# A two-block transformer forward pass: the second block's modulation vectors as multiply-and-sum instructions on VectorE in the feed-forward parts, in place of matmuls on TensorE in the mixing stages

## The chip, the core and the metric

The kernel runs on one core of a Trainium2 chip. Its engines are named as the profile names them: PE is TensorE (PEld its weight loads), DVE is VectorE, ACT is ScalarE, POOL is GpSimd, SP is SyncE, which here only issues DMAs. Each engine works through one queue of instructions in order; engines wait for one another by semaphores. The metric is the device time of one execution in microseconds (us).

## What is computed

Two transformer blocks on 512 tokens of width 1024, in fp32. The first block has two layers, each a feed-forward, a mixing stage (attention over selected keys, RWKV-7 and a gated delta net side by side) and a second feed-forward. The second block has two layers with adaptive layer norms: latent attention and a feed-forward, then Fourier mixing and a feed-forward. The change concerns the modulation vectors of these norms, which depend on `c` and `c_ctx` (one vector of 1024 each) and on weights alone, not on the tokens:

```python
def ada(cvec, w, b):                       # cvec [1, 1024], w [1024, 6144]
    return jnp.split(jax.nn.silu(cvec) @ w + b, 6, axis=-1)
...
for i in range(DEPTH):                     # DEPTH = 2
    sh1, sc1, g1, sh2, sc2, g2 = [m[:, None, :] for m in ada(c, ada_w[i], ada_b[i])]
    csh1, csc1, cg1, csh2, csc2, cg2 = ada(c_ctx, ada_w[i], ada_b[i])
```

The feed-forward that occurs four times in the first block, and the mixing stage between two of them:

```python
def swiglu(h, w_gate, w_up, w_down):       # 1024 -> 2816 -> 1024
    return (jax.nn.silu(h @ w_gate) * (h @ w_up)) @ w_down
...
x = x + 0.5 * swiglu(rms_norm(x, ffn_norm[l, 0]), ffn_w_gate[l, 0], ffn_w_up[l, 0], ffn_w_down[l, 0])
... # mixing: x = x + concat(ya, yb, yc) @ w_out[l]
x = x + 0.5 * swiglu(rms_norm(x, ffn_norm[l, 1]), ffn_w_gate[l, 1], ffn_w_up[l, 1], ffn_w_down[l, 1])
```

## The kernel before, in words

Activations are kept by feature: a tile has 128 features on the partitions and 512 tokens in a row. Matmuls in fp32 are made of three fp32r matmuls, with each operand split into a high and a low part. `slab` fetches a weight block of 128x1024 (512 KB) into `wraw`, a ring of **three** buffers, by a DMA on SP's queue (L159); ACT casts it to the high part `whi` (L160), DVE subtracts for the low part `wlo` (L161), each in a ring of two; `mm3` issues the three matmuls (L167 to L169). A `wraw` buffer is free when both parts are made, a `whi` or `wlo` buffer when PE has used it.

A feed-forward (`ffn`) first walks over 11 pairs of hidden tiles `f0`, with four slabs for each (the up part, matmuls `pg`); its results are evacuated by DVE and ACT (L292 to L295, split at L172 and L173). Then `down` multiplies back to the width of 1024: two halves of the output, 11 slabs each (the down part, matmuls `pd`, 24 for a slab), and DVE adds each half to `x` (L321 before, L323 after). The first instructions of the following norm (`xh`, `xl` L215, `sq` L253) run as soon as x is ready.

The mixing stage (`Mix`) interleaves generators: `r0`, `r1` (RWKV heads), `g0`, `g1` (delta net), attention tiles and projections. The recurrences end in a chain of state steps: PE multiplies the state by two matrices (`bY` L758, `bS` L761), DVE adds the input of the chunk (`S`, L762), and the next step needs that. `stream(tag, level)` sets the priority with which a scheduler merges the pieces into each engine's queue when the kernel is built; a lower level goes earlier.

`Block2.ada` makes the modulations of one layer, as such a generator (`fill`), called four times late in `Mix`. Each of its first three pieces takes 2048 output features: for each of 8 tiles of input features two DMAs of 512 KB into the `wraw` ring (L1105), straight from the weights and not split, and four fp32 matmuls with the activations as the stationary operand, 128x32 of which two columns count (L1107); then ACT copies the bank (`adt`, L1110). The last piece transposes (`adT`, L1083) and adds the bias.

Of the kernel before, what the change touches and what calls it, by code (L numbers as in the profile page):

```python
# [9 lines left out]
F32 = mybir.dt.float32  # L10
# [71 lines left out]
_QF = [("norm1_g0", 8), ("norm1_g1", 8), ("norm2_g0", 8), ("norm2_g1", 8), ("ada_b0", 48), ("ada_b1", 48), ("cc", 16),  # L82
# [13 lines left out]
class Net:  # L96
    """Buffers and the parts that all layers share. A stream is a run of dependent work with its own buffers: tiles of one tag
    get their buffers in program order, so only work with other tags can go ahead of work that waits."""
# [22 lines left out]
    def phase(self):  # L121
        """what follows comes after all before it in priority."""
        self.base += 400000
        self.next = {}
        self.tc.cur_priority = self.base

    @contextmanager
    def stream(self, tag, level):
        """work with the buffers of tag; the lower its level the sooner an engine takes it."""
        old, pri = self.tag, self.tc.cur_priority  # L130
        key = (tag, level)
        self.tag, self.tc.cur_priority = tag, self.next.get(key, self.base + int(level * 40000))
        yield
        self.next[key] = self.tc.cur_priority
        self.tag, self.tc.cur_priority = old, pri
# [39 lines left out]
    def rsqrt(self, src, n, eps):  # L175
        """(src + eps) ** -0.5 of a [128, n] block: a guess from the bits, a step of third order and one of Newton's."""
# [5 lines left out]
        # t = v y^2, y <- y (t^2 - 10/3 t + 5): 8/3 of the root  # L182
# [4 lines left out]
        # of z = 3/8 y: z (1.5 - 0.5 v z^2)  # L187
# [6 lines left out]
    def rsqrt3(self, src, n, eps):  # L194
        """(src + eps) ** -0.5 of a [128, n] block, by Newton's iteration."""
# [11 lines left out]
    def split_x(self, x, g, level=0.002):  # L207
        """(x * g) in two fp32r parts; the rms factor of x over the features, on all partitions and by token."""
# [14 lines left out]
    def rms(self, acc, ones, nt, eps, tag=None, copy=True):  # L223
        """rsqrt of the mean over the partitions of the sum of acc, [128, nt*128] each: by token, and on all partitions."""
# [31 lines left out]
    def split_mod(self, x, G, sh, w=T, r=None):  # L256
        """rms_norm(x) * G + sh in two fp32r parts."""
# [17 lines left out]
    def ffn(self, x, xs, wg, wu, wd, scale, pre=iter(())):  # L275
# [3 lines left out]
        for f0 in range(0, NF, 2):  # L279
# [9 lines left out]
            for i in range(2):  # L289
# [15 lines left out]
    def down(self, x, hh, hl, w, order, scale, banks=(("a", "a", "x", "x"), ("pj", "pj", "c", "c"))):  # L305
# [19 lines left out]
class Mix:  # L325
    """Sequence mixing of one layer of the first block. Streams: "w" projections, "c" the recurrences one after the other,
    "a" index scores and attention."""

    def __init__(self, net, l, x, par, w_in, lup, v_down, v_up, w_out, vfirst, fill):
# [16 lines left out]
        def go(part, tag="c", level=0):  # L346
            """the next piece of a part."""
# [27 lines left out]
        go(fill, "w", 1.25)  # L375
        go(fill, "w", 4)
# [28 lines left out]
    def proj_fm(self, c0, n=128):  # L405
        """[n, T] of rms_norm(x) @ w_in[:, c0:c0+n]."""
# [9 lines left out]
    def proj_tm(self, c0, evac, tiles=range(4)):  # L416
        """256 columns by token, before the rms factor: evac(t, [128, 256])."""
# [32 lines left out]
    def rope_tables(self, g):  # L450
        """cos * g and (-sin * g2 | sin * g1) by token, [128, 4, 64] each."""
# [12 lines left out]
    def rope(self, x, a, b, nh, out):  # L464
        """x [128, nh*64], a, b [128, 64] -> out [128, nh, 64]."""
# [10 lines left out]
    def stack_q(self, x):  # L476
        """x [128, 512] by token -> per head [128 (hi; lo), 128] fp32r."""
# [20 lines left out]
    def index_in(self):  # L498
# [4 lines left out]
        # index keys  # L503
# [9 lines left out]
        # index weights  # L513
# [10 lines left out]
    def index(self, t):  # L524
        """additive mask of the keys that the queries of tile t attend to."""
# [21 lines left out]
    def att_in(self):  # L547
        nc, n, sm = self.nc, self.n, self.sm
        # keys and values
# [27 lines left out]
        # queries  # L577
# [120 lines left out]
        # T = X0 (I + S + S^2 + S^3), S = E X0 with the part E of L off the 16x16 blocks  # L698
# [16 lines left out]
        # queries on the state, outputs within the chunk  # L715
# [8 lines left out]
        # transition and input of each chunk  # L724
# [40 lines left out]
    def compact(self, sq, sel):  # L765
        """sums over each head's features by token: [128, (t, e)]."""
# [5 lines left out]
    def spread(self, y):  # L772
        """y [128, (t, e)] by token -> [128 (e, .), T]."""
# [62 lines left out]
    def rwkv(self, hp):  # L836
# [47 lines left out]
        # by token  # L884
# [11 lines left out]
        # products within the chunks  # L896
# [34 lines left out]
        # group norm, bonus, gate  # L931
# [30 lines left out]
    def gdn_in(self):  # L962
# [3 lines left out]
        # gates by token, columns (t, h)  # L966
# [22 lines left out]
    def gdn(self, hp):  # L989
# [31 lines left out]
        # by token  # L1021
# [10 lines left out]
        # decay between the tokens of a chunk; products within the chunks  # L1032
# [24 lines left out]
        # decay over each chunk  # L1057
# [19 lines left out]
class Block2:  # L1077
    """The second block: adaLN, latent attention with a short convolution, Fourier mixing."""
# [10 lines left out]
    def ada(self, w, l):  # L1089
        """w [2, 1024, 6144]: modulations of layer l by feature; row 0 of the products is c, row 1 the context's."""  # L1090
        nc, n = self.nc, self.n
        if l == 0:
            self.act = n.xp.tile([128, 8, 32], F32, name="act")
            nc.gpsimd.memset(self.act, 0.0)
            nc.scalar.activation(out=self.act[:, :, 0:2], in_=self.p("cc").rearrange("p (k c) -> p k c", c=2), func=AF.Silu)
            self.mod, self.G = [], []
        m = n.xp.tile([128, 2, 48], F32, name=f"mod{l}")
        o = self.p(f"ada_b{l}")
        ts = []
        for q in range(3):  # L1100
            b = n.bank("ada")
            for k in range(KD):
# [437 lines left out]
```

## Time and profile before

| | |
|---|---|
| time of the timed runs | 3619.07 us, median of 3 (3618.86 to 3620.7) |
| span of the profiled execution (it has no separate time) | 3638.3 us |
| instructions | 45508 |
| busy: PE, PEld | 3554.8 us (98%), 2861.9 us (79%) |
| busy: DVE, ACT | 1864.5 us (51%), 1281.3 us (35%) |
| moved by DMA | 349.22 MB, 96 GB/s on average |

The span is that of one execution with the profiler on; the timed runs are without it. A busy share is the mean over stages with different limits. PE's matmuls overlap in the records, so a PE that is busy all the time need not be working at its peak; the weight loads show better how much passes through it.

### The profile page before, as it was taken

Reading aid. Unit: us, or ns where it says so; the run is one execution under the profiler, and the core shown is the slowest. Engines: PE = TensorE matmul, PEld = TensorE weight load, DVE = VectorE, ACT = ScalarE, POOL = GpSimd, SP = SyncE. Lnnn points to the kernel's source line nnn. Section 1 sums busy time; section 2 is a strip of 40 time slices with the busy share of each in tenths; the row PEclk is TensorE's granted clock in tenths of the full one; section 3 lists DMA queues with packets and bytes.
Section 4 is the critical chain, followed back from the end, with each engine's and each line's share of the span. In section 5 each row is a group of like instructions: output and inputs, shape, how many; then the busy total and the mean of one; then the engine's idle time right before and its main releaser. Section 6 shows DMA issues by size and latency. Waiting matters only on the chain. (4 is left out here: it accounts for less than half of the span.)

```text
span 3638.3 us, 45508 instructions
## 1 busy us (share of the span) xinstructions
PE 3554.8 (98%) x18114; PEld 2861.9 (79%) x18114; DVE 1864.5 (51%) x3863; ACT 1281.3 (35%) x2094; POOL 82.8 (2%) x169
## 2 busy tenths in 40 slices
PE   8999999999999999999999999999999999999999
PEld 7888778568888888887856788888787888778887
DVE  4443778665443344349976544436674333444332
ACT  3322534333332233235343433325573332323221
POOL 0000010000000000001000000000000000000000
PEclk9999989999999999999999999999999999999999
DMA  4333321543333333332244333342203332233332
GB/s 140 99 99 103 98 58 44 167 143 104 93 98 99 93 99 94 109 103 65 48 143 149 116 93 97 106 123 73 59 1 96 95 99 99 64 93 87 99 99 93
DMA packets 314549, 349.22 MB, mean 96 GB/s; under 512 B 40896, under 2 KB 247904, under 8 KB 314208
## 3 DMA queue, kind: packets, MB, share of 16 engines
q1 hardware_dynamic: 314048, 346.05, 31.9%
q8 instruction: 142, 2.33, 0.3%
q14 instruction: 71, 0.58, 0.0%
q10 hardware_dynamic: 288, 0.26, 0.0%
HBM read 332.11 MB, written 14.16 MB: 95 GB/s over the span
## 5 line engine op out<-in xcount | busy, mean ns | idle before, releaser
L161 DVE TENSOR_TENSOR wlo<-wraw,whi 128x1024 fp32r<-128x1024 f32 x516 | 627.1, 1215 | 1278.8 <-ACT whi L160 1278.4
L160 ACT CAST whi<-wraw 128x1024 fp32r<-128x1024 f32 x516 | 538.7, 1044 | 1337.4 <-PE pd L168 533.5
L167 PE MATMUL pg<-xh,whi 128*128 128x512 f32 x2112 | 826.0, 392 | 14.0 <-ACT whi L160 10.8
L169 PE MATMUL pg<-xh,wlo 128*128 128x512 f32 x2112 | 825.1, 391 | 0.0
L168 PE MATMUL pg<-xl,whi 128*128 128x512 f32 x2112 | 824.8, 391 | 0.0
L167 PEld LDWEIGHTS pg<-xh,whi 128*128 128x128 f32 x2112 | 398.4, 189 | 96.6 <-ACT whi L160 10.8
L168 PEld LDWEIGHTS pg<-xl,whi 128*128 128x128 f32 x2112 | 398.3, 189 | 82.9 <-DVE xl L272 0.6
L169 PEld LDWEIGHTS pg<-xh,wlo 128*128 128x128 f32 x2112 | 397.8, 188 | 82.6 <-DVE wlo L161 0.8
L169 PE MATMUL pd<-h,wlo 128*128 128x512 f32 x1056 | 411.3, 389 | 0.0
L168 PE MATMUL pd<-h,whi 128*128 128x512 f32 x1056 | 411.2, 389 | 0.0
L167 PE MATMUL pd<-h,whi 128*128 128x512 f32 x1056 | 411.1, 389 | 0.0
L169 PEld LDWEIGHTS pd<-h,wlo 128*128 128x128 f32 x1056 | 198.3, 188 | 41.1 <-DVE wlo L161 0.2
L168 PEld LDWEIGHTS pd<-h,whi 128*128 128x128 f32 x1056 | 198.3, 188 | 41.1
L167 PEld LDWEIGHTS pd<-h,whi 128*128 128x128 f32 x1056 | 198.3, 188 | 41.0
L168 PE MATMUL pf<-xl,whi 128*128 128x512 f32 (+4 forms) x424 | 167.7, 396 | 0.5 <-DVE xl L272 0.5
L167 PE MATMUL pf<-xh,whi 128*128 128x512 f32 (+4 forms) x424 | 167.1, 395 | 0.9 <-ACT xh L271 0.9
L169 PE MATMUL pf<-xh,wlo 128*128 128x512 f32 (+4 forms) x424 | 167.0, 394 | 0.0
L293 ACT ACTIVATE t<-t 128x512 f32<-128x512 f32 x88 | 55.6, 632 | 253.3 <-DVE t L292 253.3
L172 ACT CAST h<-t 128x512 fp32r<-128x512 f32 x132 | 81.6, 620 | 130.4 <-DVE t L295 83.6
L173 DVE TENSOR_TENSOR h<-t,h 128x512 fp32r<-128x512 f32 x132 | 91.0, 691 | 71.0 <-ACT h L172 70.9
L1107 PE MATMUL ada<-wraw,act 128*32 128x512 f32 x384 | 91.0, 658 | 21.2 <-DMA wraw<-in_ada_w_dram 21.1
L168 PEld LDWEIGHTS pf<-xl,whi 128*128 128x128 f32 (+2 forms) x424 | 79.0, 186 | 20.3 <-issue 3.0
(479 smaller groups left out, 4730.7 us busy)
## 6 DMA issues: line engine op xcount, KB each, us to landing
wraw<-in_ffn_w_dram SPq DMA_DIRECT2D x132, 512.0 KB, 3.6
wraw<-in_ada_w_dram SPq DMA_DIRECT2D x96, 512.0 KB, 4.6
wraw<-in_ffn_w_gate_dram SPq DMA_DIRECT2D x88, 512.0 KB, 3.7
wraw<-in_ffn_w_up_dram SPq DMA_DIRECT2D x88, 512.0 KB, 3.7
wraw<-in_ffn_w_down_dram SPq DMA_DIRECT2D x88, 512.0 KB, 3.7
wraw<-in_w_in_dram SPq DMA_DIRECT2D x69, 512.0 KB, 3.7
wraw<-in_w_out_dram SPq DMA_DIRECT2D x16, 512.0 KB, 3.9
xd<-x SPq DMA_DIRECT2D x24, 256.0 KB, 3.7
```

The lines of the kernel that those rows point to most:

```text
L160: nc.scalar.copy(out=hi[:, :k * n], in_=raw[:, :k * n])
L161: nc.vector.tensor_sub(out=lo[:, :k * n], in0=raw[:, :k * n], in1=hi[:, :k * n].bitcast(F32))
L167: mm(out, lhsT=wh, rhs=xh, start=start, stop=False)
L168: mm(out, lhsT=wh, rhs=xl, start=False, stop=False)
L169: mm(out, lhsT=wl, rhs=xh, start=False, stop=stop)
L172: self.nc.scalar.copy(out=hi, in_=src)
L173: self.nc.vector.tensor_sub(out=lo, in0=src, in1=hi.bitcast(F32))
L293: nc.scalar.activation(out=t1, in_=t1, func=AF.Silu)
L1107: nc.tensor.matmul(b[g * 32:(g + 1) * 32], lhsT=self.act[:, k], rhs=raw[g // 2][:, (g % 2) * 512:(g % 2 + 1) * 512], start=(k == 0), stop= ...
```

## The change

The modulations of both layers are made by one generator, `ada(w, cc)`. The weights are transposed on the host so that each output feature is a row of 1024; 128 output features lie on the partitions. A step is one DMA of 512 KB into the `wraw` ring (tile `araw`: two groups of 128 features, half of the inputs) and two DVE instructions that multiply 128x512 by the activation vector, repeated on all partitions (`act`), and sum along the row. Six loads of `act` on ACT's DMA queue, each with its Silu, belong to it (L1100, L1101 after). There are 112 steps: 16 for `c_ctx` (of which only two of the six vectors of layer 0 are used), and 48 for `c` in each layer. The DMAs of the modulations move 58.7 MB where they moved 50.3 MB.

The generator is advanced by one step after each pair `f0` of the up part and after each slab of the down part, in the four feed-forwards of the first block: 11 + 22 steps in the first, second and third, 11 + 2 in the fourth. The four calls in `Mix` go. (The change also drops comments, so lines move by a few.)

```diff
     def ffn(self, x, xs, wg, wu, wd, scale, pre=iter(()), fill=iter(())):
...
                 self.split(t2, hh[-1], hl[-1])
+            next(fill, None)
         next(pre, None)
-        self.down(x, hh, hl, wd, list(range(NF)), scale)
+        self.down(x, hh, hl, wd, list(range(NF)), scale, fill=fill)
...
                     self.mm3(pb[d], wh[:, k, c], wl[:, k, c], hh[f0 + k], hl[f0 + k], i0 + k == 0, i0 + k == nk - 1)
+                next(fill, None)
...
-        go(fill, "w", 1.25)
-        go(fill, "w", 4)
         go(g0, "c", 0)
...
-        go(fill, "w", 4)
...
-        go(fill, "w", 4)
...
-    def ada(self, w, l):
...
-        for q in range(3):
-            b = n.bank("ada")
-            for k in range(KD):
-                raw = [n.wraw.tile([128, SL], F32, tag="wraw", name="wraw") for _ in range(2)]
-                for i in range(2):
-                    nc.sync.dma_start(out=raw[i], in_=w[l, k * 128:(k + 1) * 128, q * 2048 + i * 1024:q * 2048 + (i + 1) * 1024])
-                for g in (0, 2, 1, 3):
-                    nc.tensor.matmul(b[g * 32:(g + 1) * 32], lhsT=self.act[:, k], rhs=raw[g // 2][:, (g % 2) * 512:(g % 2 + 1) * 512],
-                                     start=(k == 0), stop=(k == KD - 1))
-            ts.append(n.f("adt"))
-            nc.scalar.copy(out=ts[q], in_=b)
-            yield
...
+    def ada(self, w, cc):
+        nc, n = self.nc, self.n
+        self.mod, self.G = [], []
+        for l in range(2):
+            m = n.xp.tile([128, 2, 48], F32, name=f"mod{l}")
+            o = self.p(f"ada_b{l}")
+            for c in ((0,) if l else (1, 0)):
+                nj = 16 if c else 48
+                for a in range(2):
+                    act = n.xp.tile([128, D // 2], F32, tag="act", name="act")
+                    acc = m[:, c] if a else n.xp.tile([128, 48], F32, tag="acc2", name="acc2")
+                    nc.scalar.dma_start(out=act, in_=cc[c, :, a * 512:(a + 1) * 512])
+                    nc.scalar.activation(out=act, in_=act, func=AF.Silu)
+                    for j in range(0, nj, 2):
+                        raw = n.wraw.tile([128, SL], F32, tag="wraw", name="araw")
+                        r = raw.rearrange("p (j k) -> p j k", j=2)
+                        nc.sync.dma_start(out=r, in_=w[l, j:j + 2, :, a * 512:(a + 1) * 512].rearrange("j p k -> p j k"))
+                        for i in range(2):
+                            nc.vector.tensor_tensor_reduce(out=r[:, i], in0=r[:, i], in1=act, scale=1.0, scalar=0.0,
+                                                           op0=ALU.mult, op1=ALU.add, accum_out=acc[:, j + i:j + i + 1])
+                        yield
...
-        Mix(n, l, x, par, a["w_in"][l], a["lup"][l], a["v_down"], a["v_up"], a["w_out"][l], vf, b2.ada(a["ada_w"], l))
+        Mix(n, l, x, par, a["w_in"][l], a["lup"][l], a["v_down"], a["v_up"], a["w_out"][l], vf)
...
-        "ada_w": i["ada_w_2"],
+        "ada_w": np.asarray(i["ada_w_2"]).transpose(0, 2, 1).reshape(2, 48, 128, D), "cc": np.stack([row(i["c_2"][0]), row(i["c_ctx_2"])]),
```

How the queues change is seen at three places. The first is DVE's queue in a down part, here in the first feed-forward of layer 0 before; names end in the number of the buffer's use, and what an instruction waits for stands in brackets.

```order
L161 TENSOR_TENSOR wlo_1839<-wraw_1837,whi_1838 128x1024 [waits DMAHW3_49,PE_49,Activation_49]
L161 TENSOR_TENSOR wlo_1869<-wraw_1867,whi_1868 128x1024 [waits DMAHW4_49,PE_49,Activation_49]
L161 TENSOR_TENSOR wlo_1899<-wraw_1897,whi_1898 128x1024 [waits DMAHW5_49,PE_49,Activation_49]
L161 TENSOR_TENSOR wlo_1929<-wraw_1927,whi_1928 128x1024 [waits DMAHW6_49,PE_49,Activation_49]
L161 TENSOR_TENSOR wlo_1959<-wraw_1957,whi_1958 128x1024 [waits DMAHW7_49,PE_49,Activation_49]
```

After, in the same part, two reductions (each an instruction and the read of its sum) stand between one `wlo` and the next:

```order
L161 TENSOR_TENSOR wlo_2321<-wraw_2319,whi_2320 128x1024 [waits DMAHW7_49,PE_49,Activation_49]
L1107 ISA araw_2383,acc2_2032<-araw_2383,act_2031 128x512 [waits DMAHW2_49,DVE_49]
L1107 ISA acc2_2032 128x1
L1107 ISA araw_2383,acc2_2032<-araw_2383,act_2031 128x512
L1107 ISA acc2_2032 128x1
L161 TENSOR_TENSOR wlo_2355<-wraw_2353,whi_2354 128x1024 [waits DMAHW1_49,PE_49,Activation_49]
L1107 ISA araw_2417,acc2_2032<-araw_2417,act_2031 128x512 [waits DMAHW4_49,DVE_49]
```

Nothing stood between two `wlo` before; now the reductions of `araw_2383` come ahead of the `wlo` of `wraw_2353`.

The second place is SP's queue of DMAs there. Before it held one slab after the other:

```order
L159 DMA wraw_1837<-in_ffn_w_down_dram 128x2x512 [waits DMAHW0_49,DVE_49]
L159 DMA wraw_1867<-in_ffn_w_down_dram 128x2x512 [waits DMAHW1_49,DVE_49]
L159 DMA wraw_1897<-in_ffn_w_down_dram 128x2x512 [waits DMAHW2_49,DVE_49]
L159 DMA wraw_1927<-in_ffn_w_down_dram 128x2x512 [waits DMAHW3_49,DVE_49]
L159 DMA wraw_1957<-in_ffn_w_down_dram 128x2x512 [waits DMAHW4_49,DVE_49]
```

After, slabs and modulation weights alternate:

```order
L159 DMA wraw_2319<-in_ffn_w_down_dram 128x2x512 [waits DMAHW7_49,DVE_49]
L1105 DMA araw_2349<-in_ada_w_dram 128x2x512 [waits DMAHW4_49,DVE_49]
L159 DMA wraw_2353<-in_ffn_w_down_dram 128x2x512 [waits DMAHW1_49,DVE_49]
L1105 DMA araw_2383<-in_ada_w_dram 128x2x512 [waits DMAHW2_49,DMAHW0_49,DVE_49]
L159 DMA wraw_2387<-in_ffn_w_down_dram 128x2x512 [waits DMAHW7_49,DMAHW3_49,DVE_49]
L1105 DMA araw_2417<-in_ada_w_dram 128x2x512 [waits DMAHW2_49,DVE_49]
```

In a ring of three, `araw_2383` gets the buffer that `wraw_2319` had, and `wraw_2387` that of `araw_2349`.

The third place is PE's queue in the mixing stage of layer 0, where the state steps of `r1` are. Before:

```order
L758 MATMUL bY_5027<-RT_3940,S_5036 128x64
L761 MATMUL bS_5047<-S_5036,M_4079 128x128
L1107 MATMUL ada_5820<-wraw_5870,act_5816 32x512
L1107 MATMUL ada_5820<-wraw_5869,act_5816 32x512
L1107 MATMUL ada_5820<-wraw_5870,act_5816 32x512
L758 MATMUL bY_5027<-RT_3940,S_5037 128x64
L761 MATMUL bS_5051<-S_5037,M_4080 128x128
L612 MATMUL s_6173<-kh0_4595,qs_6154 128x256
L613 MATMUL s_6173<-kl0_4597,qs_6154 128x256
L758 MATMUL bY_5027<-RT_3940,S_5037 128x64
L761 MATMUL bS_5055<-S_5037,M_4080 128x128
```

After (L756 and L759 are the same two lines):

```order
L756 MATMUL bY_5173<-RT_4086,S_5182 128x64
L759 MATMUL bS_5193<-S_5182,M_4225 128x128
L756 MATMUL bY_5173<-RT_4086,S_5183 128x64
L759 MATMUL bS_5197<-S_5183,M_4226 128x128
L1052 MATMUL G_5390<-KQ_5303 128x256
L756 MATMUL bY_5173<-RT_4086,S_5183 128x64
L759 MATMUL bS_5201<-S_5183,M_4226 128x128
```

The `ada` matmuls are gone from between the steps; a matmul of the delta net stands in one gap.

## Rows read from the trace of the kernel before

**Rows 1.** The page: busy times, and PEld's busy tenths in 40 slices.

```profile
PE 3554.8 (98%) x18114; PEld 2861.9 (79%) x18114; DVE 1864.5 (51%) x3863; ACT 1281.3 (35%) x2094; POOL 82.8 (2%) x169
...
PEld 7888778568888888887856788888787888778887
```

**Rows 2.** The page's groups: busy us, mean ns | idle before, releaser.

```profile
L1107 PE MATMUL ada<-wraw,act 128*32 128x512 f32 x384 | 91.0, 658 | 21.2 <-DMA wraw<-in_ada_w_dram 21.1
```

**Rows 3.** The tile `ada`: idle us and times until a release.

```profile
  DMA wraw<-in_ada_w_dram: 51.5, 49
```

**Rows 4.** Windows in layer 0's mixing: PE, PEld, DVE, ACT, POOL busy, PEclk, DMA.

```profile
560.00:600.00 40.00, 38.65 (x447) 33.88 (x446) 33.29 (x76) 15.96 (x36) 5.97 (x10) 1.00 0.10 28
...
660.00:680.00 20.00, 17.08 (x79) 8.71 (x79) 12.24 (x39) 5.76 (x9) 1.69 (x3) 0.83 0.59 173
```

**Rows 5.** DVE's timeline, `r0`: first and last of six state steps (start, duration).

```profile
597.97 0.28 DVE L762 TENSOR_TENSOR S<-bS,B 128x128 f32<-128x128 f32 x1
...
604.34 0.29 DVE L762 TENSOR_TENSOR S<-bS,B 128x128 f32<-128x128 f32 x1 [0.20 <-PE bS L761]
```

**Rows 6.** DVE's timeline, `r1`: first and last of six state steps.

```profile
665.04 0.28 DVE L762 TENSOR_TENSOR S<-bS,B 128x128 f32<-128x128 f32 x1
...
676.67 0.29 DVE L762 TENSOR_TENSOR S<-bS,B 128x128 f32<-128x128 f32 x1 [0.93 <-PE bS L761]
```

**Rows 7.** PE's timeline there (in brackets the wait before).

```profile
669.70 1.93 PE L1107 MATMUL ada<-wraw,act 128*32 128x512 f32 x6 [2.43 <-DMA wraw<-in_ada_w_dram]
...
674.32 1.67 PE L1107 MATMUL ada<-wraw,act 128*32 128x512 f32 x2
...
676.79 1.06 PE L1107 MATMUL ada<-wraw,act 128*32 128x512 f32 x6
```

**Rows 8.** DVE's groups by form.

```profile
L292 DVE TENSOR_TENSOR t<-pg,rstd 128x512 f32<-128x512 f32 x88 | 60.3, 686 | 23.8 <-PE pg L169 23.7
...
L614 DVE CUSTOM_DVE_ANT_0 p<-s,msk 128x512 f32<-128x512 f32 x16 | 10.9, 689 | 4.9 <-PE s L613 4.8
```

**Rows 9.** DVE's timeline around one such product, in layer 1's attention.

```profile
2031.69 0.69 DVE L614 CUSTOM_DVE_ANT_0 p<-s,msk 128x512 f32<-128x512 f32 x1 [0.63 <-PE s L613]
2032.30 0.08 DVE L614 DVE_READ_ACCUMULATOR2_ANT sx<- 128x1 f32 x1
```

**Rows 10.** Timelines of DVE, ACT, SP and PE, first feed-forward, at the down part's start.

```profile
257.64 1.22 DVE L161 TENSOR_TENSOR wlo<-wraw,whi 128x1024 fp32r<-128x1024 f32 x1
...
262.92 1.23 DVE L161 TENSOR_TENSOR wlo<-wraw,whi 128x1024 fp32r<-128x1024 f32 x1 [2.08 <-ACT whi L160]
268.36 1.23 DVE L161 TENSOR_TENSOR wlo<-wraw,whi 128x1024 fp32r<-128x1024 f32 x1 [4.21 <-ACT whi L160]
...
267.27 1.05 ACT L160 CAST whi<-wraw 128x1024 fp32r<-128x1024 f32 x1 [4.39 <-PE pd L168]
...
264.17 0.37 SPq L159 DMA_DIRECT2D wraw<-in_ffn_w_down_dram  x1
...
267.71 0.39 PE L169 MATMUL pd<-h,wlo 128*128 128x512 f32 x1
```

**Rows 11.** DMA issues: KB each, median us from issue to landing.

```profile
wraw<-in_ada_w_dram SPq DMA_DIRECT2D x96, 512.0 KB, 4.6
...
wraw<-in_ffn_w_down_dram SPq DMA_DIRECT2D x88, 512.0 KB, 3.7
...
wraw<-in_w_out_dram SPq DMA_DIRECT2D x16, 512.0 KB, 3.9
...
wraw<-in_w_o_dram SPq DMA_DIRECT2D x8, 512.0 KB, 3.4
...
x<-in_xT_dram SPq DMA_DIRECT2D x8, 256.0 KB, 4.8
```

**Rows 12.** DVE's timeline at the boundary of the halves: first and last of ten.

```profile
312.97 1.41 DVE L321 SCALAR_TENSOR_TENSOR x<-pd,x 128x512 f32<-128x512 f32 x2
...
320.73 0.68 DVE L253 TENSOR_TENSOR sq<-sq 128x512 f32<-128x512 f32 x1
```

More of the change, by code (lines that the diff above doesn't have):

```diff
@@ L301, in ffn, with down @@
                 self.split(t2, hh[-1], hl[-1])
+            next(fill, None)
         next(pre, None)
-        self.down(x, hh, hl, wd, list(range(NF)), scale)
-    def down(self, x, hh, hl, w, order, scale, banks=(("a", "a", "x", "x"), ("pj", "pj", "c", "c"))):
+        self.down(x, hh, hl, wd, list(range(NF)), scale, fill=fill)
+    def down(self, x, hh, hl, w, order, scale, banks=(("a", "a", "x", "x"), ("pj", "pj", "c", "c")), fill=iter(())):
         nc = self.nc
@@ L1087, in p @@
         return self.par[:, o:o + n]
-    def ada(self, w, l):
+    def ada(self, w, cc):
         nc, n = self.nc, self.n
[L1092 to L1099, printed above, removed]
-        for q in range(3):
-            b = n.bank("ada")
-            for k in range(KD):
-                raw = [n.wraw.tile([128, SL], F32, tag="wraw", name="wraw") for _ in range(2)]
-                for i in range(2):
-                    nc.sync.dma_start(out=raw[i], in_=w[l, k * 128:(k + 1) * 128, q * 2048 + i * 1024:q * 2048 + (i + 1) * 1024])
-                for g in (0, 2, 1, 3):
-                    nc.tensor.matmul(b[g * 32:(g + 1) * 32], lhsT=self.act[:, k], rhs=raw[g // 2][:, (g % 2) * 512:(g % 2 + 1) * 512],
-                                     start=(k == 0), stop=(k == KD - 1))
-            ts.append(n.f("adt"))
-            nc.scalar.copy(out=ts[q], in_=b)
-            yield
-        for q, t in enumerate(ts):
-            b = n.bank("adT")
-            for i in range(4):
-                self.tr(b[:, i * 128:(i + 1) * 128], t[:, i * 128:(i + 1) * 128])
-            for c in range(2):
-                j = slice(q * 16, (q + 1) * 16)
-                v = lambda a: a.rearrange("p (g i) -> p g i", g=4)
-                nc.vector.tensor_add(out=v(m[:, c, j]), in0=b.rearrange("p (i g r) -> p g i r", i=4, g=4)[:, :, :, c], in1=v(o[:, j]))
-        self.mod.append(m)
-        G = n.xp.tile([128, 3, 8], F32, name=f"G{l}")
-        for i, (c, j, nm) in enumerate(((0, 1, "norm1_g"), (0, 4, "norm2_g"), (1, 1, "norm1_g"))):
-            nc.vector.scalar_tensor_tensor(out=G[:, i], in0=m[:, c, j * 8:(j + 1) * 8], scalar=1.0, in1=self.p(f"{nm}{l}"),
-                                           op0=ALU.add, op1=ALU.mult)
-        self.G.append(G)
@@ new lines, in ada @@
+        self.mod, self.G = [], []
[17 more added lines that the diff above has]
+                        yield
+                    if not a:
+                        first = acc
+                nc.vector.tensor_add(out=m[:, c, :nj], in0=m[:, c, :nj], in1=o[:, :nj])
+                nc.vector.tensor_add(out=m[:, c, :nj], in0=m[:, c, :nj], in1=first[:, :nj])
+            self.mod.append(m)
+            G = n.xp.tile([128, 3, 8], F32, name=f"G{l}")
+            for i, (c, j, nm) in enumerate(((0, 1, "norm1_g"), (0, 4, "norm2_g"), (1, 1, "norm1_g"))):
+                if l == 0 or c == 0:
+                    nc.vector.scalar_tensor_tensor(out=G[:, i], in0=m[:, c, j * 8:(j + 1) * 8], scalar=1.0, in1=self.p(f"{nm}{l}"),
+                                                   op0=ALU.add, op1=ALU.mult)
+            self.G.append(G)
@@ L1463 @@
     b2 = Block2(n, par2)
+    fill = b2.ada(a["ada_w"], a["cc"])
     for l in range(2):
@@ L1468 @@
             n.phase()
[L1469 removed]
+        n.ffn(x, n.split_x(x, P("ffn_norm0"), 0.002 if l else .006)[0], a["ffn_w_gate"][l, 0], a["ffn_w_up"][l, 0], a["ffn_w_down"][l, 0], 0.5, fill=fill)
         n.phase()
[L1471 removed]
+        Mix(n, l, x, par, a["w_in"][l], a["lup"][l], a["v_down"], a["v_up"], a["w_out"][l], vf)
         n.phase()
         n.ffn(x, n.split_x(x, P("ffn_norm1"))[0], a["ffn_w_gate"][l, 1], a["ffn_w_up"][l, 1], a["ffn_w_down"][l, 1], 0.5,
[L1474 removed]
+              b2.context(a["ctxT"]) if l else iter(()), fill)
     n.phase()
@@ L1518, in _layout @@
         "ffn_w_gate": i["ffn_w_gate"], "ffn_w_up": i["ffn_w_up"], "ffn_w_down": i["ffn_w_down"],
-        "ada_w": i["ada_w_2"], "w_in_2": i["w_in_2"][0], "w_uq": i["w_uq_2"][0], "w_ukv": i["w_ukv_2"][0], "w_o": i["w_o_2"][0],
+        "ada_w": np.asarray(i["ada_w_2"]).transpose(0, 2, 1).reshape(2, 48, 128, D), "cc": np.stack([row(i["c_2"][0]), row(i["c_ctx_2"])]), "w_in_2": i["w_in_2"][0], "w_uq": i["w_uq_2"][0], "w_ukv": i["w_ukv_2"][0], "w_o": i["w_o_2"][0],
         "w_fourier": i["w_fourier_2"][0], "ffn_w1": i["ffn_w1_2"], "ffn_w3": i["ffn_w3_2"], "ffn_w2": i["ffn_w2_2"],
```

16 lines of the change are left out of this document (7 added, 9 removed).

## The prediction

> **What bounds the kernel now.** I read the page from the top. The busy lines and the slices [rows 1] show TensorE (PE) occupied 98% of the span, VectorE (DVE) 51%. The line of weight loads (PEld) says more: 7 to 8 tenths in the feed-forward stretches, 5 to 6 in slices 7, 8, 20 and 21, the second halves of the two mixing stages, where PE is occupied but moves less. These are the slices of the removed work. The table of costly groups has it in one line [rows 2]: 384 records of 128x512 matmuls (two for each of the program's 2 × 24 × 4 = 192), 91.0 us of PE, and 21.2 us of idle time ahead of them, nearly all until a weight DMA. The view of the tile adds PE and its weight loads together and finds 49 such waits [rows 3]. So at most 91.0 + 21.2 = 112 us of PE time can go.
>
> Whether that time is on the path is read from windows and from the timeline. In a 40 us window of mixing ahead of the modulations PE and DVE are nearly full, 38.65 and 33.29 us, the clock 1.00; in 660 to 680 DVE has 12.24 of 20 us and the clock is 0.83 [rows 4]. So here neither engine is full: a chain runs back and forth between them, the delta rule's state steps (PE L758 and L761, then DVE L762). Without modulations between them five steps take 604.34 − 597.97 = 6.37 us [rows 5]; with them, the same number takes 676.67 − 665.04 = 11.63 us [rows 6], 5.26 longer. In that stretch PE shows 2.43 us of waiting, then 1.93 us of `ada`, then 1.67 us [rows 7], 6.03 in all: 5.26/6.03 = 87% of it is lost to the chain.
>
> **What the removal gives.** Upper bound: all 112 us. A second, tighter one: 87% everywhere, 0.87 × 112 = 98 us. Lower bound: only the 5.26 us shown, and as much in the other layer: 10 us, if all other modulation matmuls filled holes. The shown step is a place where the chain is bare; elsewhere attention and projections offer PE other work, and DVE's 12.24 of 20 us [rows 4] sets a floor that isn't far below. With no row for the rest I take the middle of 10 and 98, 54, and go a little up, to **60 us**, since the DMA waits (21.2) stop PE whatever it might have done next. The twelve transposes and three evacuations of a layer go with it, and are in the rounding.
>
> **What is added.** 224 reductions on DVE and 112 DMAs of 512 KB, in the four feed-forward parts of the first block: 33, 33, 33 and 13 steps. A reduction's price: the trace has the attention's product with a sum over 128x512, 689 ns [rows 8], and an accumulator read of 0.08 us; the read, and with it the next instruction, starts 2032.30 − 2031.69 = 0.61 us after it [rows 9]. Two cost 1.22 us (at most 1.54, the full durations), 137 us in all, on an engine that is half idle. That alone would be free.
>
> In the up parts it is: one step falls to four slabs (21.8 us of PE), DVE's share grows by 1.3 of 21.8, and no slab's `wlo` is delayed by more than one reduction or two. I put these at nothing; the cover is the lead shown next, about 3 us.
>
> The down parts are another matter. Before, the loop is paced by PE: `whi` (ACT) waits 4.39 us for `pd`, casts in 1.05, DVE waits 4.21, makes `wlo` in 1.23, and so every 268.36 − 262.92 = 5.44 us [rows 10]. `wlo` of 262.92 is done at 264.15, and the first matmul that needs that slab's `wlo` starts 267.71 [rows 10]: a lead of 3.56 us. The freed raw buffer is refilled at once (issue at 264.17, 0.02 later [rows 10]).
>
> After, the order on DVE is: reduction pair n+1, then `wlo` n+1; and a raw buffer of the ring of three is shared. `araw_2383` takes the buffer of `wraw_2319`, which is free when `wlo_2321` is done; its reductions stand **ahead of** `wlo_2355`, whose slab landed long ago. So each `wlo` starts one DMA, and the next `wlo` waits for that DMA and two reductions. The loop: 0.02 to the issue, landing, about 0.04 to the reductions (an estimate), 1.22, and `wlo` 1.23. The landing of a slab of this shape takes 3.7 us in the down part, 3.9 for the output projection's, issued close behind each other, 4.6 for the modulations' pairs [rows 11]. After, the slab's own DMA goes out 1.2 us ahead of the modulations', so I take the middle row, 3.9: 0.02 + 3.9 + 0.04 + 1.22 + 1.23 = **6.41 us** against PE's 5.44: 0.97 us late per slab. Bounds: 3.4 us to land, the least of a slab's rows [rows 11], gives 5.91, so 0.47; 4.6 and 1.54 for the reductions give 7.43, so 1.99.
>
> The lead doesn't save it for long: it is gone at the start of the part. Ahead of the second slab's `wlo` stand there, after the first one's, a DMA, its reductions and six operations of the last evacuation (0.69 us long [rows 8], 0.61 from start to start [rows 9]): 0.02 + 3.9 + 0.04 + 1.22 + 6 × 0.61 + 1.23 = 10.07 us from end to end, where it took 264.15 − 258.87 = 5.28 [rows 10]. The first one is itself late by one pair that ran ahead of it, 1.42 with its gaps (an estimate). 10.07 − 5.28 + 1.42 − 3.56 of lead = 2.65 us left over. At the boundary of the two halves the updates of x, the split and the squares, which filled DVE from 312.97 to 321.41 before [rows 12], come between the reductions and the next two `wlo`, and each pair's DMA still starts only after the `wlo` before: some 6 us of them on two slabs, less about 1 that fits into the landings; I take 5 (0 to 8.4). In each down part the vector `act` is loaded anew once, ahead of a cast on ACT's queue; I take 1.2 us (0 to 4.8, a 256 KB load [rows 11]). Per down part: 20 × 0.97 + 2.65 + 5 + 1.2 = 28.3 us; three of them 85. The fourth feed-forward has two steps there: 0 to 3, taken as 0. At the start `act` and the first reductions lie ahead of the first activations: 3 us (0 to 4.8). Sum of the losses: **88 us** (bounds 3 × 20 × 0.47 = 28 and 3 × (20 × 1.99 + 2.65 + 8.4 + 4.8) + 3 + 4.8 = 175).
>
> **The sum.** The profiled execution's span, the only time it has, is 3638.3 us and would become 3638.3 − 60 + 88 = 3666; it lies 19.2 above the median of the timed runs, which was measured without a profile. On that median: 3619.1 − 60 + 88 = **3647 us**.
>
> A rule against this arrangement: the Trainium skill, "Perfetto Trace Analysis", section "Identifying Performance Opportunities", holds that the same gap repeating on the engine that should be saturated can mean too few buffers for the next tile. The trace of before shows no such gap in the down parts, with the same three buffers; by the rule it comes as soon as two streams share them, as in my sum.
>
> **Rivals.**
> - *Faster: the DMA is no link of the loop.* If the landing and DVE fit in 5.44 us (a landing under 2.9 us), the lead of 3.56 us stays and the added work is covered. For it: DVE's idle 4.21 us per slab is more than 1.22. Against it: no slab's row is below 3.4 [rows 11]. The loss is then the starts and boundaries, 15 us or less: 3619 − 60 + 15 = 3574. In a milder form the mixing gives 90 and the loop takes 5.91 us with half of the starts and boundaries: 3619 − 90 + 28 + 15 = 3572. 0.20 for both.
> - *Same.* Gain and loss cancel, e.g. 75 against 75: 3619. It needs a landing of about 3.75 and a gain near the upper bound. 0.14.
> - *Slower still: the mixing stages are held by something else.* With 10 to 25 us of gain: 3619 − 20 + 88 = 3687. For it: DVE is full in the stretch ahead [rows 4]; against it, the state steps [rows 6]. 0.14.
> - *Slower still: the clock.* After the wait of 2.43 us six matmuls took 1.93 us, later six took 1.06 [rows 7]: a wait was followed by the lower of the two levels (1.2 and 2.4 GHz). If PE's new waits in the down parts did that to a tenth of the 66 slabs, each would take 5.44 us longer: 36 us, 3683. Against it: the new waits are 1 to 4 us, most near 1, and a window with short gaps is at 1.00 [rows 4]. 0.06. The Trainium skill's page "TensorE: Matmul & The Clock Gate", section "HAM oscillation — how this bites in real kernels", describes such a kernel, where waits for DMA between bursts throttle the clock again and again; by it every stalled slab could pay.
> - *My own case*: the loop at 6.2 to 6.8 us and a gain of 40 to 80: 3628 to 3675. 0.46.
>
> **How the numbers follow.** Two runs of this kernel can be told apart from about 0.2%, 7.2 us. Faster (below 3612): the first rival, 0.20. Same: the second, 0.14. Slower: my case and the two slower rivals, 0.46 + 0.14 + 0.06 = 0.66. The range: from the far side of the "same" case, taking in a part of the faster one (3597), to the slower rivals' time, 3690; outside are the greater part of the first rival and the largest bounds of the loop, about 0.2. My case's own range is 3628 to 3675.
>
> **What would show it.** Right: in the down parts of the first three feed-forwards `wlo` and casts come every 6.3 to 6.5 us, PE's `pd` group idles about 0.9 us per slab behind `wlo` (60 to 80 us in all), and DVE waits on the modulations' DMA; the up parts keep 21.8 us per four slabs; each mixing stage is some 30 us shorter. Wrong: `pd` without idle time (a landing near 3 us, or reductions that found their data there); mixing stages shortened by under 15 or over 45 us; a granted clock below 1.00 in the down parts; DVE's reductions above 0.75 us each.

## The result, and the profile after

The changed kernel takes 3585.25 us (median of 4, 3579.58 to 3596.89) where the kernel before takes 3619.89 us: a ratio of 0.9894, with a 95% interval of 0.9872 to 0.9917. It is 35 us faster; the forecast was 28 us slower, with a range that began at 3597.

Below are lines of the page of the changed kernel: busy times, the weight loads' slices (both answer to [rows 1]), the clock's slices, the reductions' group (in the place of [rows 2]) and two DMA issues (beside [rows 11]).

```profile
PE 3485.7 (97%) x17706; PEld 2866.3 (80%) x17706; DVE 2001.2 (56%) x4304; ACT 1284.0 (36%) x2094; POOL 83.7 (2%) x168
...
PEld 7888778678888888887867788888787888778887
...
PEclk9999979899999999999989999999999999999999
...
L1107 DVE CUSTOM_DVE_ANT_0 araw<-araw,act 128x512 f32<-128x512 f32 x224 | 148.9, 688 | 179.9 <-DMA araw<-in_ada_w_dram 171.5
...
araw<-in_ada_w_dram SPq DMA_DIRECT2D x112, 512.0 KB, 3.5
...
wraw<-in_ffn_w_down_dram SPq DMA_DIRECT2D x88, 512.0 KB, 4.2
```

A reduction takes 688 ns, as priced. VectorE stood idle ahead of the reductions for 171.5 us until a modulation DMA; that it would wait on these DMAs was forecast, that nobody would wait for VectorE there was not. The next table, worked out from the timelines, has the time from the last `pd` matmul of each layer's first feed-forward to the first `pg` of the second (the mixing stage with the norms on both sides), and the down parts, from first to last `pd`.

```
              mixing 0  mixing 1   down parts, four feed-forwards
before          492.1     483.0    119.8  119.8  119.8  121.7
changed         467.2     454.9    120.3  119.8  119.8  122.9
```

The mixing stages are 24.9 and 28.1 us shorter, the down parts together 1.7 us longer, and the first up part 0.6. The sum of these, 51 us, is more than the 35 us of the timed runs, because the profiled execution of the kernel before was long (3638.3 us); the first experiment comes back to that.

Why the down parts lose nothing is seen in DVE's, SP's and ACT's timelines of the changed kernel, in the first down part:

```profile
279.88 0.69 DVE L1107 CUSTOM_DVE_ANT_0 araw<-araw,act 128x512 f32<-128x512 f32 x1
280.49 1.22 DVE L161 TENSOR_TENSOR wlo<-wraw,whi 128x1024 fp32r<-128x1024 f32 x1
284.27 0.69 DVE L1107 CUSTOM_DVE_ANT_0 araw<-araw,act 128x512 f32<-128x512 f32 x1 [2.56 <-DMA araw<-in_ada_w_dram]
...
285.50 1.22 DVE L161 TENSOR_TENSOR wlo<-wraw,whi 128x1024 fp32r<-128x1024 f32 x1
289.13 0.69 DVE L1107 CUSTOM_DVE_ANT_0 araw<-araw,act 128x512 f32<-128x512 f32 x1 [2.41 <-DMA araw<-in_ada_w_dram]
...
280.60 0.37 SPq L1105 DMA_DIRECT2D araw<-in_ada_w_dram  x1
281.74 0.37 SPq L159 DMA_DIRECT2D wraw<-in_ffn_w_down_dram  x1
285.62 0.37 SPq L1105 DMA_DIRECT2D araw<-in_ada_w_dram  x1
...
289.21 1.06 ACT L160 CAST whi<-wraw 128x1024 fp32r<-128x1024 f32 x1 [4.38 <-PE pd L168]
294.65 1.05 ACT L160 CAST whi<-wraw 128x1024 fp32r<-128x1024 f32 x1 [4.38 <-PE pd L168]
```

The second reduction that starts at 279.88 is done at 280.57, and the next modulation DMA is issued at 280.60; the slab's DMA is issued at 281.74, when `wlo` (280.49 + 1.22) is done. The next pair does the same (its second reduction ends at 285.58, the DMA goes out at 285.62), and so does the one after it (290.43 and 290.47). So the modulations' tile gets back its *own* buffer, not the slab's: by these releases `araw_2349`, `araw_2383` and `araw_2417` all lie in one of the three, and the slabs alternate in the other two. The sentence in the section on the change that gives `araw_2383` the buffer of `wraw_2319` is wrong. The loop is then issue, landing and two reductions, with `wlo` inside the landing: 289.13 − 284.27 = 4.86 us, less than PE's 5.44, and the casts come every 294.65 − 289.21 = 5.44 us, paced by `pd` as in [rows 10].

In the mixing stage, the six state steps of `r1` on DVE's timeline, first and last (they answer to [rows 6]):

```profile
652.04 0.28 DVE L760 TENSOR_TENSOR S<-bS,B 128x128 f32<-128x128 f32 x1
...
658.66 0.29 DVE L760 TENSOR_TENSOR S<-bS,B 128x128 f32<-128x128 f32 x1 [0.20 <-PE bS L759]
```

Five steps take 6.62 us, near the 6.37 of [rows 5] and far from the 11.63 of [rows 6]. But the windows of that stage (columns as in [rows 4]), of before and then of the changed kernel, show what came in its place:

```profile
640.00:680.00 40.00, 36.34 (x180) 19.30 (x175) 27.82 (x90) 14.37 (x33) 1.69 (x3) 0.91 0.59 179
680.00:720.00 40.00, 35.53 (x199) 21.52 (x198) 26.24 (x123) 16.76 (x44) 0.42 (x2) 0.91 0.52 166
720.00:760.00 40.00, 35.99 (x271) 22.08 (x270) 26.71 (x88) 10.76 (x31) 4.12 (x6) 1.00 0.43 133
```

```profile
640.00:680.00 40.00, 31.34 (x162) 22.84 (x161) 34.34 (x104) 21.47 (x46) 1.87 (x3) 0.81 0.14 41
680.00:720.00 40.00, 34.02 (x229) 29.21 (x230) 35.38 (x144) 14.18 (x40) 3.78 (x7) 0.85 0.13 26
720.00:760.00 40.00, 35.80 (x342) 31.65 (x339) 30.85 (x98) 14.89 (x40) 4.48 (x6) 0.87 0.05 8
```

Without the modulations PE is idle for longer, and its granted clock in these three windows, 0.91–1.00 before, is 0.81–0.87. Single windows vary between executions (0.51, 0.98 and 0.96 in a second profile of the changed kernel), so the whole mixing stages are the better measure: 0.951 and 0.972 before (0.958 and 0.975 in a second profile), 0.909 and 0.940 in the changed kernel (0.933 and 0.915). A larger part of the time is at the lower level, 1.2 GHz, so part of the freed time may go into slower matmuls; the last experiment tests that.

### The profile page after: what moved, and what is told of

It is laid out like the page before. It is cut to its first block, busy times and chain, and to the rows that moved or that the text cites. A ratio compares the mean times of both kernels' runs of the same rounds, so it can differ in the third digit from the quotient of the medians.

```text
span 3584.8 us, 45235 instructions
## 1 busy us (share of the span) xinstructions
PE 3485.7 (97%) x17706; PEld 2866.3 (80%) x17706; DVE 2001.2 (56%) x4304; ACT 1284.0 (36%) x2094; POOL 83.7 (2%) x168
## 4 chain that ended last, share of the span: by engine, by line
PE 89%; DVE 7%; ACT 2%; issue 1%; DMA 1%; POOL 0%; SPq 0%; DVEq 0%; ACTq 0%; POOLq 0%
PE pg L167 13%; PE pg L169 13%; PE pg L168 13%; PE pd L167 8%; PE pd L168 8%; PE pd L169 8%; PE pf L168 2%; PE pf L169 2%; PE pf L167 2%; PE lv L692 2%; PE pT L1367 1%; PE G L905 1%; PE pT L624 1%; DVE wlo L161 1%; PE pt L429 1%
## 5 line engine op out<-in xcount | busy, mean ns | idle before, releaser
L1107 DVE CUSTOM_DVE_ANT_0 araw<-araw,act 128x512 f32<-128x512 f32 x224 | 148.9, 688 | 179.9 <-DMA araw<-in_ada_w_dram 171.5
L167 PEld LDWEIGHTS pf<-xh,whi 128*128 128x128 f32 (+2 forms) x424 | 79.5, 187 | 17.5 <-ACT xh L271 1.0
```

The lines of the kernel that those rows point to most:

```text
L167: mm(out, lhsT=wh, rhs=xh, start=start, stop=False)
L1107: nc.vector.tensor_tensor_reduce(out=r[:, i], in0=r[:, i], in1=act, scale=1.0, scalar=0.0, op0=ALU.mult, op1=ALU.add, accum_out=acc[:, j + ...
```

## The experiments

Theory 1: the gain is the removal of PE's waits for modulation data, which stop everything behind them on PE's queue, and the matmuls' own 91 us [rows 2] cost little. Rival: the 91 us of PE time was the gain. For the down parts: a loop of 4.9 us that runs beside PE, against my forecast's loop of 6.41. The expectations name theories by letters of their own. Ratios are to the kernel before, run on the same chip. The first run is the changed kernel a second time.

> The changed kernel again, to be compared with the next one on one chip: 0.989 of the kernel before.

It was 0.9889 (0.9857 to 0.9921), and its mixing stages took 456.3 and 464.2 us in the profile.

**The kernel before, profiled again** (no edit).

> The kernel before, unchanged, for a second profile. Its first profiled execution had a span of 3638 us, some 18 us above its timed runs, while the changed kernel's had 3585, like its timed runs. If the first profile was of a slow execution, this one's span is near 3618 and each of the two mixing stages (from the last pd matmul of the first feed-forward to the first pg of the second) is 8 to 10 us shorter than the 492 and 483 us there. If the profiler itself adds the time, the span is again about 3638.

It took 3631.95 us, its span was 3630.2 us, and the mixing stages 486.9 and 479.9 us: the length varies from one execution to the next (timed runs of this kernel went from 3613.75 to 3643.81 over the chips used). The feed-forwards did not vary. The profiles' difference in the mixing stages, 45 to 53 us, is thus somewhat too large; for a size the timed ratios are better.

**No modulation work at all**

```diff
+                    nc.vector.tensor_copy(out=acc[:, :nj], in_=act[:, :nj])
                     for j in range(0, nj, 2):
-                        raw = n.wraw.tile([128, SL], F32, tag="wraw", name="araw")
-                        ...
-                        nc.sync.dma_start(out=r, ...)
-                        for i in range(2):
-                            nc.vector.tensor_tensor_reduce(out=r[:, i], ...)
                         yield
```

> The changed kernel without its 112 weight DMAs and 224 reductions (the modulations are then wrong: they are the activation vector's first columns plus the bias). My prediction's theory: the added work costs 88 us, so this runs at 3585 - 88 = 3497. Theory from the changed kernel's trace, where the four feed-forwards take the same time as before within 1.2 us: the added work costs 0 to 5 us, so 3580 to 3585.

0.9873 (0.9853 to 0.9892), 3575.14 us: 6 to 8 us below the changed kernel by the ratios, with intervals that overlap. The added work costs about that or less, not 88 us.

**The matmuls of before, from a resident tile**

```diff
-                raw = [n.wraw.tile([128, SL], F32, tag="wraw", name="wraw") for _ in range(2)]
-                for i in range(2):
-                    nc.sync.dma_start(out=raw[i], ...)
...
-                    nc.tensor.matmul(..., rhs=raw[g // 2][:, (g % 2) * 512:(g % 2 + 1) * 512],
+                    nc.tensor.matmul(..., rhs=n.cst[:, :512],
```

> The kernel before with its modulation matmuls in place, but fed from a resident tile (their 96 DMAs are left out, so the modulations are wrong). Theory A, the gain came from the waits for those DMAs (21 us of PE idle time): about 3619 - 21 = 3598 or less, near the changed kernel. Theory B, the gain came from the matmuls' own PE time: about 3610 to 3619, and removing them as well gives the rest. If it is below 3585, the matmuls themselves are worth more than they cost, by the clock: then PE's granted clock in the mixing stages is near 1.00 here, where the changed kernel has 0.66 to 0.96.

0.9904 (0.9883 to 0.9926). With all 192 matmuls still in the mixing stages the kernel before gains as much as the change does. These windows show a granted clock of 0.93 to 1.00:

```profile
640.00:680.00 40.00, 38.62 (x251) 19.30 (x243) 31.68 (x126) 20.19 (x45) 1.34 (x2) 1.00 0.10 26
680.00:720.00 40.00, 37.42 (x319) 29.33 (x319) 30.02 (x97) 13.86 (x36) 4.71 (x8) 0.93 0.13 26
720.00:760.00 40.00, 37.43 (x311) 29.64 (x311) 30.14 (x108) 16.30 (x42) 2.92 (x5) 0.98 0.05 8
```

Against the kernel with neither (0.9873), the matmuls cost 0.3%, about 11 us; the intervals just overlap. But two things changed with the waits. The same matmuls occupy PE for 54.1 us here, not 91.0. And the scheduler merged the queues anew: in layer 0 the modulation matmuls stand in 36 groups over 169 us of PE's queue before, here in 21 groups over 63 us. So this run takes away the waits and moves the matmuls, and doesn't say which of the two counts.

**The DMAs of before, with little matmul time**

```diff
+                    w_ = 16 if k else 512
-                    nc.tensor.matmul(b[g * 32:(g + 1) * 32], ..., rhs=raw[g // 2][:, (g % 2) * 512:(g % 2 + 1) * 512],
+                    nc.tensor.matmul(b[g * 32:(g + 1) * 32, :w_], ..., rhs=raw[g // 2][:, (g % 2) * 512:(g % 2) * 512 + w_],
```

> The kernel before with its 96 modulation DMAs, but with 168 of its 192 modulation matmuls cut from 512 to 16 columns (the modulations are wrong). Feeding the matmuls from a resident tile had brought 36 us, leaving out everything 45 to 48. Theory A, what the modulations cost in the mixing stages is their DMAs, by PE's waits for them and by the delta net's own scratch DMAs that stand behind them on SP's queue: the time stays at 3605 to 3620. Theory B, it is PE time: 3575 to 3590.

0.9981 (0.9963 to 0.9999): theory A, the DMAs, and not the rival's PE time. The modulation matmuls occupy PE for 32.9 us in place of 91.0, still spread over some 150 us in layer 0, and the time hardly moves. A part of what the shorter matmuls give may be hidden by the clock, which is 0.967 to 0.976 in the timed runs (0.982 to 0.990 before). PE's waits in layer 0 (us, times, longest) are still there, beside 10.8 us before:

```profile
PE ada L1108 <- DMA wraw<-in_ada_w_dram: 9.1, 9, 3.2
```

**The same bytes, but nobody waits for them.** The edit is that of the resident tile, with the DMAs kept.

> The kernel before with its 96 modulation DMAs of 512 KB in the mixing stages and its matmuls, but the matmuls read a resident tile (the modulations are wrong): PE waits for no modulation DMA and no such DMA waits for PE, while the bytes still move and the delta net's scratch DMAs still share the queue. Without the DMAs these matmuls had run at 0.990 of the kernel before. Theory P, the cost is PE's waits for the data: again about 0.990. Theory Q, it is the transfers themselves (scratch DMAs land later, and go out later behind them on SP's queue): 0.995 to 1.000.

0.9881 (0.9861 to 0.9900): theory P. The delta net's scratch DMAs in layer 0 land no sooner than before (KB, us to landing; before it was 2.7 and 3.8), and VectorE waits longer for one of them (8.1 us in the whole run, 4.1 before), yet that costs nothing to be seen:

```profile
s<-GA SPq DMA_DIRECT2D x8, 128.0 KB, 2.8
...
d<-s SPq DMA_DIRECT2D x2, 64.0 KB, 5.0
...
DVE GA L688 <- DMA s<-GA: 8.1, 5, 4.1
```

Nor is it their place behind the modulations' DMAs on SP's queue: the latest of the 16 `s<-GA` DMAs goes out 1.6 us after its `GA` is done before (652.00, 653.62), and 3.0 us here (1826.61, 1829.64). As with the resident tile alone, the matmuls (56.4 us of PE) also moved, as the tile's records by 40 slices of the span show, before and then here (overlapping records are added up):

```profile
busy tenths in 40 slices 0000000860000000000087100000000000000000
```

```profile
busy tenths in 40 slices 0000000900000000000091000000000000000000
```

**The same waits, for a sixteenth of the bytes**

```diff
-                    nc.sync.dma_start(out=raw[i], in_=w[l, ..., q * 2048 + i * 1024:q * 2048 + (i + 1) * 1024])
+                    nc.sync.dma_start(out=raw[i][:, :64], in_=w[l, ..., q * 2048 + i * 1024:q * 2048 + i * 1024 + 64])
...
+                                     rhs=bc(raw[g // 2][:, 0:64].rearrange("p (o c) -> p o c", o=1), [128, 8, 64])
```

> The kernel before with each modulation DMA cut to a sixteenth (64 of 1024 columns, which the matmuls read eight times over; the modulations are wrong). All instructions and waits are as before, but a transfer lands in about 2 us instead of 4.6. Theory P: PE's waits shrink from 21 us by more than half, and the time falls to 0.990 to 0.995. If the queue order on SP (each such DMA waits for PE, the scratch DMAs behind it) were what costs, it would stay at 0.997 to 1.000.

0.9928 (0.9908 to 0.9947). The DMAs land after 1.7 us, PE's waits shrink to a quarter (21.1 us before), and some two thirds of the gain are there. The matmuls stay apart here, in 36 groups over 123 us of layer 0, and occupy 79.4 us of PE. So most of the gain comes without bunching them; for the rest, waits and places are not told apart. The landing and PE's waits:

```profile
wraw<-in_ada_w_dram SPq DMA_DIRECT2D x41, 32.0 KB, 1.7
...
PE ada L1107 <- DMA wraw<-in_ada_w_dram: 5.5, 8, 1.4
```

**The modulations' DMAs on POOL's queue** (`nc.sync.dma_start` becomes `nc.gpsimd.dma_start` in `ada` of before).

> The kernel before with the modulation DMAs issued from POOL's queue instead of SP's; nothing else changes. Theory A1, the delta net's scratch DMAs are held up behind the modulations' on SP's in-order queue: 10 to 25 us faster than before, and the scratch DMAs go out as soon as their data are there. Theory A2, they are slow because all transfers share the same DMA engines (s from GA lands after 2.7 us before, 1.8 in the changed kernel), or PE's own waits cost the time: within 5 us of before.

1.0116 (1.0086 to 1.0146), slower, which neither theory had. POOL now waits for PE's modulation matmuls ahead of its own work for the delta net (layer 0):

```profile
POOL wraw L1105 <- PE ada L1107: 127.9, 23, 22.2
...
POOL DG L726 <- DVE XT L679: 38.4, 1, 38.4
```

So it says nothing about SP's queue; the two runs before it do.

**The reductions twice**

```diff
+                        for i in range(2):
+                            nc.vector.tensor_tensor_reduce(out=r[:, i], in0=r[:, i], in1=act, scale=1.0, scalar=0.0,
+                                                           op0=ALU.mult, op1=ALU.add, accum_out=scr[:, i:i + 1])
                         yield
```

> The changed kernel with each pair of reductions done twice, the second time into a scratch sum that nobody reads; no DMA is added. Theory E, in the down parts a loop of landing (3.5 us) and reductions (1.22 us) runs beside PE, 4.9 us against PE's 5.44, and the second pair makes it about 6.1 to 6.2: PE is 0.7 us late at each of some 60 slabs, 30 to 45 us in all, 3615 to 3630. Theory F, VectorE is half idle there and takes it: within 5 us of the changed kernel, 3580 to 3590.

0.9914 (0.9890 to 0.9937): not told apart from the changed kernel by its time. But the profile has the loop: the down parts take 127.5, 126.7, 125.7 and 124.1 us, 21 us more than in the changed kernel, and PE waits for `wlo` in the first of them, which it did not before:

```profile
L169 PE MATMUL pd<-h,wlo 128*128 128x512 f32 x176 | 69.9, 397 | 4.2 <-DVE wlo L161 4.1
```

So VectorE's idle share does not cover everything there: 1.22 us more for each step use up the margin. The loss is two thirds of what I expected at the least, since in the merged order the second pair often stands behind `wlo`. In the timed runs it is partly hidden by the scatter of the mixing stages.

**Three buffers strictly in turn** (`raw` hands out three tags with one buffer each, by a counter).

```diff
+    def raw(self, name):
+        self.nraw += 1
+        return self.wraw.tile([128, SL], F32, tag=f"wraw{self.nraw % 3}", name=name, bufs=1)
```

> The changed kernel with the three raw buffers handed out strictly in turn, as my prediction had assumed (in the changed kernel the modulations' tiles keep one of the three in the down parts). My prediction's loop, each wlo starting one DMA for which the next wlo waits: 60 to 85 us slower than the changed kernel, 3645 to 3670. Against it: the order of the instructions adapts, two wlo and then two pairs of reductions, so that one landing falls to two slabs (3.5 + 2 x 1.22 + 2 x 1.23 = 8.4 us for 10.9 of PE): no loss, 3580 to 3590.

0.9913 (0.9889 to 0.9937); the down parts take 124.8, 128.9, 123.7 and 123.3 us, 18 us more than in the changed kernel. Lines of VectorE in the first down part:

```profile
286.50 1.22 DVE L166 TENSOR_TENSOR wlo<-wraw,whi 128x1024 fp32r<-128x1024 f32 x1
292.81 0.69 DVE L1112 CUSTOM_DVE_ANT_0 araw<-araw,act 128x512 f32<-128x512 f32 x1 [5.09 <-DMA araw<-in_ada_w_dram]
...
293.43 1.22 DVE L166 TENSOR_TENSOR wlo<-wraw,whi 128x1024 fp32r<-128x1024 f32 x1
...
305.17 2.50 DVE L166 TENSOR_TENSOR wlo<-wraw,whi 128x1024 fp32r<-128x1024 f32 x2
```

The loop of the forecast is there, with 293.43 − 286.50 = 6.93 us from one `wlo` to the next behind a landing. But the order on VectorE changes with the buffers, and in places two `wlo` follow on one landing (305.17). So even with the assignment that I had assumed, the loss is a fifth of mine.

**Useless matmuls to keep PE occupied**, 24 in each mixing stage of the changed kernel.

```diff
+        for q in range(3):
+            b = n.bank("dum")
+            for k in range(KD):
+                nc.tensor.matmul(b[0:32], lhsT=n.cst[:, 0:32], rhs=n.cst[:, 0:512], start=(k == 0), stop=(k == KD - 1))
+            yield
```

> The changed kernel with 24 useless fp32 matmuls of 128x512 by 32 columns in each mixing stage, where the modulations' 96 had been (their result is not used). Theory C, the changed kernel loses part of the gain because PE, with more idle time between the state steps, gets the lower clock there (granted 0.66 to 0.96 in 40 us windows, 0.91 to 1.00 before): the clock rises and the time falls, by up to 20 us, to 3565 to 3580. Theory D, the lower clock costs nothing since the chain through VectorE sets the time there: the 48 matmuls add 0 to 23 us, 3585 to 3608.

0.9860 (0.9837 to 0.9882). Because it lies so near the changed kernel, it was run once more beside it:

> The changed kernel with the 48 useless matmuls, a second time, beside the changed kernel. Theory C (they keep the clock up): 0.986 again, 0.003 below the changed kernel or more. Theory D: the first result was scatter, and the two agree within 0.002.

0.9866 (0.9844 to 0.9887), 3570.59 us. Its windows in layer 0:

```profile
640.00:680.00 40.00, 40.00 (x170) 19.75 (x170) 32.30 (x125) 19.07 (x43) 1.70 (x3) 1.00 0.10 28
680.00:720.00 40.00, 36.69 (x301) 30.94 (x300) 30.59 (x101) 13.20 (x36) 4.84 (x8) 0.91 0.11 23
720.00:760.00 40.00, 38.29 (x335) 31.56 (x334) 30.42 (x108) 17.46 (x44) 4.18 (x6) 1.00 0.05 8
```

Twice it came out lower than the changed kernel (0.9894, 0.9889), by 0.2 to 0.3%, 8 to 12 us, but each pair's intervals overlap, and the second difference, 0.0023, lies between what theories C and D allow. That the clock rises with these matmuls is shown: over the timed runs it is 0.984 to 0.990, where the changed kernel has 0.969 to 0.982. That it makes the kernel faster is likely and not shown. It is the fastest version tried.

## Why the prediction was wrong

- **The loop of the down parts** is the step that failed, with 85 of the 88 us of loss. I read from the order that the modulations' reductions stand ahead of `wlo`, which holds, and added that `araw` takes the buffer freed by the `wlo` before, so that one landing and both kinds of DVE work follow one another: 6.41 us. The pool gave `araw` its own buffer; the loop is 4.86 us, with `wlo` inside the landing, and `pd` idles 0.1 us in the first down part. All the added work costs about 6 to 8 us (0.9894 and 0.9889 against 0.9873), not 88. I also took the order on VectorE as fixed: with the buffers strictly in turn it changes, and the loss is 18 us. Whether two pieces of work share a buffer is not in the names or in the size of a pool; it is in the addresses, or in what a DMA issue waits for. The landing was also shorter, 3.5 us, not 3.9.
- **The start of the parts, the boundary of the halves, `act`**: 2.65, 5 and 1.2 us each time, the first two built on the same assumption. VectorE does wait 3.47 us for `act` in the first down part (until 279.26), at no cost to PE. All together show as 0.5 us in the first down part, 0.0 in the next two and 1.2 in the fourth (which I took as 0). The lead of 3.56 us is regained, since the loop is shorter than PE's slab.
- **The gain of 60 us** had the right kind. In the profiles the mixing stages gave 53 us (45 against the second profile of before), in the timed runs the whole change 35, and the kernel with no modulation work 46 (0.9873). It came out lower, and my way to it was wrong in one point: the bound of 98 us, from which I took the middle, prices PE time and waits alike. By the runs the waits weigh far more: without them 34 to 43 us are gained with all matmuls in place (0.9904, 0.9881), and with them, but 58 us less of matmul time, 7 us (0.9981). Without waits the matmuls cost about 3 to 11 us (0.9881 and 0.9904 against 0.9873), in the 54 to 56 us of PE that they take there. How much of the gain is the waits themselves, and how much the places that the matmuls got with them, stays open. The clock works against the gain: in the timed runs without these matmuls' PE time it is 0.967 to 0.982, before 0.982 to 0.991. It was already in the 5.26 us from which I took the 87%: from 669.7 to 675.6 us PE was granted 0.50, and that price holds slower state steps as well as waits.
- **A reduction's price** (0.61 us from start to start, 688 ns) and **the up parts at nothing** were right; they take 242.5 to 242.6 us before and after, all but the first (0.6 more).
- **The rival of an unhidden clock** was placed in the down parts, where the clock stayed at 1.00 (a window from 250 to 370 us); it belonged in the mixing stages (0.951 and 0.972 before, 0.909 and 0.940 after). The rival "the DMA is no link of the loop" gave 3574 and was the right mechanism in the main, since the added work is covered, but for another reason than a short landing.
- The rule on repeating gaps and too few buffers, from the Trainium skill's "Perfetto Trace Analysis", section "Identifying Performance Opportunities", did not come into play: `pd` idles 0.1 us in the changed kernel's first down part. With the buffers strictly in turn, gaps did come: `pd` idles 3.0, 6.3 and 2.4 us behind `wlo` in the first three down parts.

## What to carry to other kernels

Before costing a loop through a shared pool, look at which buffer a tile really gets: the release that a DMA's issue follows decides whether two pieces of work run one after the other or side by side. An instruction on an in-order engine that waits for a DMA can cost more than the idle time ahead of it: here 34 to 43 us went with the waits (0.9904 and 0.9881; the matmuls' places changed as well), where the rows show 21 us of idle PE. An edit to one group of instructions can re-merge all queues, so compare the order before calling a difference the effect of that edit. Where PE's queue has holes, price its work by what removing it does to the chain and the clock, not by its busy time.

## What the runs showed of the hardware that was not expected

- In stretches of small matmuls with many short waits, leaving out 96 fp32 matmuls of a stage lowered the granted clock of the stage from 0.951–0.975 to 0.909–0.940 (two profiles each), and 24 useless ones brought it to 0.938–0.977. The Trainium skill's "Perfetto Trace Analysis", section "Matmul Optimizations", says that power is scaled by utilization and that matmuls should come back to back; these stages agree.
- With the clock the length of a mixing stage varied between executions of one program: 467.2 us at 0.909 and 454.9 at 0.940 in one profile of the changed kernel, 456.3 at 0.933 and 464.2 at 0.915 in another, while the up parts and the first three down parts agreed to half a microsecond.
- A DMA of 32 KB landed after 1.7 us where one of 512 KB took 4.6 to 4.7 in the same place.
